# Forty-four in-projections of a hybrid mLSTM, RWKV-7 and S5 step: seventeen beside the RWKV columns, twenty-three behind the last one, four behind the S5 branch's last transposes

## The chip, the cores and the metric

One NeuronCore of one Trainium2 chip runs one launch of the kernel. The metric is the time of the device for that launch in microseconds, the median of three runs: 1379.0 us (1373.04 to 1379.88). Beside the runs there is one execution taken by the hardware profiler. The engines are called PE (TensorE, matrix products), DVE (VectorE), ACT (ScalarE), POOL (GpSimd) and SP (SyncE, whose queue issues all transfers of this kernel). Each engine executes its own instructions in a fixed order.

## The reference, cut to what matters

The layer takes 512 prompt rows and 8 sample rows of width 1024. One combined projection `w_in` gives the columns of three mixers and of three merge gates; each mixer's output is gated, projected, weighted by its merge gate and summed:

```python
z = x @ p['w_in']
xm, ig, fg, og, zm, rcols, zr, u, zs, gm = _split_cols(z)
y_m = (mlstm(xm, ig, fg, og) * silu(zm)) @ p['w_bm']
y_r = (rwkv7(rcols) * silu(zr)) @ p['w_br']
ys  = gelu(s5(u)); ys = ys * sigmoid(ys @ p['s_glu_w'] + p['s_glu_b'])
y_s = (ys * silu(zs)) @ p['w_bs']
g = sigmoid(gm).reshape(b, t, 3, D)
x_new = layer_norm(ALPHA * x + (g[:,:,0]*y_m + g[:,:,1]*y_r + g[:,:,2]*y_s) @ p['w_out'])
```

RWKV-7 updates a matrix state token by token; the kernel computes it in chunks of 64 tokens, with a triangular inverse of each chunk and then eight chunks one behind the other. S5 is a complex diagonal scan in groups of 16 channels. All arrays are float32; outputs are also the new states of each mixer, for prompt and samples.

## The kernel before, in words

The normalised input lies in SBUF as two parts `xh` and `xl` (a rounded part and the rest), 1024 rows deep by 520 columns (512 + 8). One in-projection of 128 columns of `w_in` is `inproj`: it loads a weight tile in two transfers of 256 KB (`wraw`, three buffers), splits it on ACT into `whi` and on DVE into `wlo` (two buffers each), and makes two groups of 24 matmuls into the PSUM tile `g` (three buffers), for 256 and for 264 columns.

The work goes through these stages: entry norm; RWKV; S5 beside the merge of the RWKV branch (`mrg.other(1)`); mLSTM beside the S5 branch's GLU and merge (`mrg.s5()`); the mLSTM branch's merge; the last projection and norm. `interleave` emits two generators in turns.

In-projections whose results are needed only later are called fills. The list `fills` holds them in order, `fill()` takes the first one from it, and each computes a tile in a small pool `fl` (tag `fl`, two buffers) and stores it to DRAM: the S5 input `u` (`fill_u`, to `ud`) or a gate or input column (`fill_z`, tile `zf`, to `zsave`). There are 44: eight of `u`, eight each of `C_OG`, `C_ZS`, `C_ZM` and of the S5 merge gate `C_GM + 2 * D`, two of `C_XM`, two of `C_GM + D`. Later stages look a column up in the dictionary `zsave` and load it, or project it there if it is missing.

RWKV takes 25 columns of its own (`rcol`): one for the low-rank parts, then for each of the eight column tiles a key, a receptance and a value column (8 + ct, ct, 16 + ct). The inner `rcol` calls `e.fill()` ahead of each, so 25 fills are emitted beside these columns. Two column tiles are a pair: `elementwise` for both, then `inverse` (62 DVE operations on the tile `xi`, then small matmuls), then `chain`, eight steps of matmuls (`cr`, `cy`) with DVE and ACT between them, then `headnorm` and the store `ybsave`. Behind the last pair stand the samples' state update and `e.fill(len(e.fills))`, which emits the 19 that remain.

The order of instructions on each engine isn't that of the text alone. A planner with a timeline of its own takes, for each engine, the ready instruction that was emitted first, and waits between engines are added to that order. `tc.issue_after(ins)` adds an edge: what its block emits on the engine of `ins` is queued behind `ins`. Pools of SBUF are stacked from the left, or from the right with `side="right"`; a new pool's tile waits for those tiles that had its place.

S5 works on four parts `pi` of 16 groups; in each, for two halves `j`, two transposes into the PSUM tile `kt` are the last step of making a kernel `ko`, which goes through DMA into `tms`; behind them come `bu`, the scans on DVE, and the `ys` matmuls, whose result is stored to `yssave` and loaded again as `yb` for the GLU (`ysh`, `ysl`).

Of the kernel before, what the change touches and what calls it, by code (L numbers as in the profile page):

```python
# [8 lines left out]
F32 = mybir.dt.float32  # L9
# [6 lines left out]
P = 128  # L16
D = 1024
T = 512
NB = 8
N = T + NB  # L20
KT = D // P
# [11 lines left out]
EH = math.exp(-0.5)  # L33

C_XM, C_IG, C_FG, C_OG, C_ZM = 0, 1024, 1028, 1032, 2056
C_RC, C_ZR, C_U, C_ZS, C_GM = 3080, 6280, 7304, 8328, 9352


@with_exitstack
def hybrid_step(ctx: ExitStack, tc: tile.TileContext, I, O):  # L40
    nc = tc.nc
    V, A, G, TE = nc.vector, nc.scalar, nc.gpsimd, nc.tensor
# [4 lines left out]
    dr = ctx.enter_context(tc.tile_pool(name="dr", bufs=1, space=DRAM))  # L47
# [218 lines left out]
    hmsave = dr.tile([KT, P, N], F32, name="hmsave")  # L266
    ud = dr.tile([KT, P, SL, 80], F32, name="ud")
    flc = ExitStack()
    fl = flc.enter_context(tc.tile_pool(name="fl", bufs=1))
    zsave, fills = {}, []  # L270

    def fill_u(ct):
        us = fl.tile([P, SL, 80], F32, tag="fl", bufs=2, name="us")
# [28 lines left out]

    for ct in range(KT):
        fills.append((fill_u, ct))
    for b, c0 in enumerate((C_OG, C_ZS, C_ZM, C_GM + 2 * D)):
        zd = dr.tile([KT, P, N], F32, name=f"zsave{b}")
        for ct in range(KT):
            fills.append((fill_z, (c0 + ct * P, zd[ct])))

    zx = dr.tile([KT, P, N], F32, name="zsave5")  # L310
    for ct in range(2):
        fills.append((fill_z, (C_XM + ct * P, zx[ct])))

    zd = dr.tile([KT, P, N], F32, name="zsave4")
    for ct in range(2):
        fills.append((fill_z, (C_GM + D + ct * P, zd[ct])))

    def fill(k=1):
        for _ in range(k):
# [39 lines left out]

    env = dict(locals())  # L360
    rwkv(tc, I, O, env)
    flc.close()
    mrg = Merge(tc, I, O, env)
    weng[:] = [V, V]
    mrg.open("mr", 1, 4)
    interleave(s5(tc, I, O, env), mrg.other(1), 1.5)
    mrg.pctx.close()
    weng[:] = [V, V]
    mrg.open("ms", 1, 4)
    interleave(mlstm(tc, I, O, env), mrg.s5(), 0.42)  # L370
    mrg.pctx.close()
    mrg.open("mf", 3, 5)
    for _ in mrg.other(0, ahead=True):
        pass
# [6 lines left out]
def interleave(a, b, n):  # L381

    due = 0.0
    for _ in a:
        due += n
        while due >= 1:
            next(b, None)
            due -= 1
    for _ in b:
        pass  # L390


def rwkv(tc, I, O, env):
    e = type("E", (), env)
    nc = tc.nc
    V, A, G, TE = nc.vector, nc.scalar, nc.gpsimd, nc.tensor
    dma, pa, pc, mm, tr, pcol, inproj, gemm = e.dma, e.pa, e.pc, e.mm, e.tr, e.pcol, e.inproj, e.gemm
    ctx = ExitStack()
    rl = ctx.enter_context(tc.tile_pool(name="rl", bufs=1))
    dr, par, col, epst, shn = e.dr, e.par, e.col, e.epst, e.shn  # L400
# [17 lines left out]
    def rt(name, tag="t", bufs=TB):  # L418
        return rp.tile([P, N], F32, tag=tag, bufs=bufs, name=name)

    def rcol(j):
        rc = rp.tile([P, 1 + N], F32, tag="rc", bufs=1, name="rc")
        e.fill()
        return e.rcol(j, rc, rt("xr"))


# [275 lines left out]
    for s_ in range(4):  # L702
# [11 lines left out]
        for ci in range(2):  # L714
            ct = 2 * s_ + ci
# [6 lines left out]
    for j in range(2):  # L722
        m = 128 if j == 0 else 97
        p = pa("sf")
# [68 lines left out]
    V.tensor_tensor(yst, yst, lng, op=ALU.mult)  # L793
    V.tensor_tensor(bf, bf, yf, op=ALU.add)
    dma(e.ybsave[:, :, T:N].rearrange("c p b -> p c b"), bvs)
    e.fill(len(e.fills))
    ctx2.close()
    ctx.close()
    e.weng[:] = [V, V]
# [145 lines left out]
def s5(tc, I, O, env):  # L945
# [20 lines left out]
    for pi in range(KT // 2):  # L966
# [48 lines left out]
        for j in range(2):  # L1015
            c0 = g0 + 8 * j
            eb = sp.tile([P, 8, SL, SC], F32, tag="eb", bufs=2, name="eb")
            et = sp.tile([P, 8, SL, SC], F32, tag="et", bufs=2, name="et")
            pw = lambda t, q, lo_: t[:, q, lo_:lo_ + SL, c0:c0 + 8].rearrange("p s g -> p g s").unsqueeze(3).to_broadcast(sh)
            bx = lambda q: bb[:, q, 8 * j:8 * j + 8].unsqueeze(2).to_broadcast(sh)  # L1020
            V.tensor_tensor(eb, pw(pf, 0, 0), bx(0), op=ALU.mult)
            V.tensor_tensor(et, pw(pf, 1, 0), bx(1), op=ALU.mult)
            V.tensor_tensor(eb, eb, et, op=ALU.add)
            gm = sp.tile([P, 8, SL, SC], F32, tag="gm", bufs=2, name="gm")
            cx = lambda q: ca[:, j, q].unsqueeze(2).to_broadcast(sh)
            V.tensor_tensor(gm, pw(pf, 0, 1), cx(0), op=ALU.mult)
            gt = sp.tile([P, 8, SL, SC], F32, tag="et", bufs=2, name="gt")
            V.tensor_tensor(gt, pw(pf, 1, 1), cx(1), op=ALU.mult)
            V.tensor_tensor(gm, gm, gt, op=ALU.add)


            p = pa("ko")
            for m in range(4):
                mm(p[32 * m:32 * m + 32, 0:2 * P], ca[:, j, 0, 2 * m:2 * m + 2, :].rearrange("p g c -> p (g c)"),
                   eb[:, 2 * m:2 * m + 2].rearrange("p g s c -> p (g s c)"))
            kt = sp.tile([P, 2, P], F32, tag="w4", bufs=6, name="kt")
            A.activation(kt.rearrange("p h c -> p (h c)"), p[:, 0:2 * P], AF.Copy)
            p = pa("kt")
            for h in range(2):
                tr(p[:, h * P:(h + 1) * P], kt[:, h])  # L1040
            for h in range(2):
                A.activation(ko[:, j].rearrange("p (m h c) -> p m h c", h=2, c=SC)[:, :, h],
                             p[:, h * P:(h + 1) * P].rearrange("p (m h c) -> p m h c", h=2, c=SC)[:, :, h], AF.Copy)
            gms.append(gm)
            ebs.append(eb)
        kf = ko.rearrange("p j c -> p (j c)")
        V.tensor_tensor(kf[0:SC], kf[0:SC], dm.rearrange("p g c -> p (g c)"), op=ALU.add)
        for t in range(SL):
# [695 lines left out]
```

## Time and profile before

| | |
|---|---|
| median of three runs | 1379.0 us |
| the profiled execution | 1378.35 us |
| its span, first to last instruction | 1376.3 us |
| mean granted clock of TensorE | 0.947 of 2.4 GHz |
| PE matmul busy | 1254.4 us, 91% of the span, 10509 instructions |
| PE weight load busy | 1147.4 us, 83% |
| DVE busy | 959.2 us, 70%, 2157 instructions |
| ACT busy | 679.5 us, 49%, 1492 instructions |
| POOL busy | 242.8 us, 18% |
| moved by DMA | 168.49 MB, mean 122 GB/s |

Busy times are unions of the instructions' spans on one engine. Matmuls are pipelined and their ends are modelled, so two that follow each other overlap in the record; how dense they are is read from their starts. The granted clock is 1.0 at 2.4 GHz and 0.5 at 1.2 GHz; a mean between them says for which part of a stretch either held. A wait is put down to the engine and line whose signal came last.

### The profile page before, as it was taken

Reading aid. Unit: us, or ns where it says so; the run is one execution under the profiler, and the core shown is the slowest. Engines: PE = TensorE matmul, PEld = TensorE weight load, DVE = VectorE, ACT = ScalarE, POOL = GpSimd, SP = SyncE. Lnnn points to the kernel's source line nnn. Section 1 sums busy time; section 2 is a strip of 40 time slices with the busy share of each in tenths; the row PEclk is TensorE's granted clock in tenths of the full one; section 3 lists DMA queues with packets and bytes.
Section 4 is the critical chain, followed back from the end, with each engine's and each line's share of the span. In section 5 each row is a group of like instructions: output and inputs, shape, how many; then the busy total and the mean of one; then the engine's idle time right before and its main releaser. Section 6 shows DMA issues by size and latency. Waiting matters only on the chain.

```text
span 1376.3 us, 27658 instructions
## 1 busy us (share of the span) xinstructions
PE 1254.4 (91%) x10509; PEld 1147.4 (83%) x10509; DVE 959.2 (70%) x2157; ACT 679.5 (49%) x1492; POOL 242.8 (18%) x396
## 2 busy tenths in 40 slices
PE   4969999999998999999985988996999999999887
PEld 4969988889897889999865988996989888899855
DVE  6694594569357834768836998995776775555857
ACT  4547657465746674453222332334765774453220
POOL 1402211123122311105200020000000011104600
PEclk8989999999999999999977999997999999999999
DMA  6333332213121312354518444546676866465331
GB/s 185 95 91 109 91 97 64 74 50 87 52 78 46 89 55 85 96 147 141 160 29 149 110 97 104 130 99 179 208 225 207 275 200 203 138 201 189 92 107 62
DMA packets 246707, 168.49 MB, mean 122 GB/s; under 512 B 54808, under 2 KB 222106, under 8 KB 246302
## 3 DMA queue, kind: packets, MB, share of 16 engines
q1 hardware_dynamic: 246574, 166.72, 43.0%
q8 instruction: 83, 1.36, 0.4%
q14 instruction: 50, 0.41, 0.1%
HBM read 125.18 MB, written 39.20 MB: 119 GB/s over the span
## 4 chain that ended last, share of the span: by engine, by line
PE 35%; DVE 7%; DMA 5%; issue 2%; SPq 2%; ACT 1%; POOL 0%; DVEq 0%; ACTq 0%; POOLq 0%
PE g L62 23%; PE qk L62 2%; PE ys L62 2%; DVE wlo L131 2%; SPq L53 2%; PE s L62 1%; DMA wraw<-in_w_bm_dram 1%; PE nd L62 1%; PE pn L62 1%; PE v L62 1%; DMA cn<-in_state_mlstm_c_dram 1%; PE cn L62 1%; DMA wraw<-in_w_out_dram 1%; DMA br<-in_s_b_im_dram 1%; PE cy L62 1%
## 5 line engine op out<-in xcount | busy, mean ns | idle before, releaser
L62 PE MATMUL g<-xh,whi 128*128 128x264 f32 (+1 forms) x1552 | 461.2, 297 | 37.8 <-DVE th L1541 16.0
L62 PE MATMUL g<-xl,whi 128*128 128x264 f32 (+1 forms) x1552 | 457.1, 295 | 2.1 <-DVE xl L217 2.1
L62 PE MATMUL g<-xh,wlo 128*128 128x264 f32 (+1 forms) x1552 | 454.8, 293 | 0.2 <-DVE wlo L131 0.2
L62 PEld LDWEIGHTS g<-xh,whi 128*128 128x128 f32 x1552 | 304.4, 196 | 48.5 <-DVE th L1541 17.0
L62 PEld LDWEIGHTS g<-xl,whi 128*128 128x128 f32 x1552 | 304.2, 196 | 5.3 <-DVE xl L217 2.3
L62 PEld LDWEIGHTS g<-xh,wlo 128*128 128x128 f32 x1552 | 303.6, 196 | 4.4 <-issue 1.1
L130 ACT ACTIVATE whi<-wraw 128x512 fp32r<-128x512 f32 x258 | 151.2, 625 | 201.0 <-PE g L62 154.3
L131 DVE TENSOR_TENSOR wlo<-wraw,whi 128x512 fp32r<-128x512 f32 x258 | 197.5, 788 | 75.4 <-ACT whi L130 72.9
L661 DVE SCALAR_TENSOR_TENSOR xv<-xv,pc,cy 64x64 f32<-64x64 f32 x112 | 31.3, 279 | 28.1 <-PE cy L62 25.3
L62 PE MATMUL g<-ysh,whi 128*128 128x256 f32 (+1 forms) x128 | 39.1, 312 | 11.5 <-ACT ysh L258 9.1
L564 DVE TENSOR_TENSOR lr<-gg,maskg 64x256 f32<-64x256 f32 x32 | 13.5, 422 | 47.4 <-ACT la L563 47.3
L601 DVE TENSOR_TENSOR xi<-xi,itmp 128x31 f32<-128x31 f32 (+15 forms) x124 | 42.7, 344 | 3.0
L62 PE MATMUL g<-w_bmh,wlo 128*128 128x264 f32 (+1 forms) x128 | 37.4, 293 | 7.8 <-DVE wlo L131 7.6
L599 DVE TENSOR_TENSOR itmp<-lu,xi 128x31 f32<-128x31 f32 (+15 forms) x124 | 42.2, 340 | 2.9
L647 POOL COPY xv<-yv 64x128 f32<-64x128 f32 x64 | 24.7, 388 | 109.1 <-PE cr L62 53.8
L62 PE MATMUL g<-w_brh,whi 128*128 128x256 f32 (+1 forms) x128 | 37.4, 295 | 2.8 <-DVE mg L1585 2.6
L62 PE MATMUL g<-ysl,whi 128*128 128x256 f32 (+1 forms) x128 | 39.7, 311 | 0.0
L62 PE MATMUL g<-ysh,wlo 128*128 128x256 f32 (+1 forms) x128 | 39.3, 307 | 0.0
L568 POOL TENSOR_SCALAR_AFFINE_SELECT ar<-ar 64x512 f32<-64x512 f32 x32 | 21.2, 664 | 94.8 <-ACT ar L567 72.8
L62 PE MATMUL g<-bsl,whi 128*128 128x264 f32 (+1 forms) x128 | 37.8, 297 | 0.0
L62 PE MATMUL g<-bsh,wlo 128*128 128x256 f32 (+1 forms) x128 | 37.6, 295 | 0.0
L62 PEld LDWEIGHTS g<-ysh,whi 128*128 128x128 f32 x128 | 26.3, 209 | 13.4 <-ACT ysh L258 9.4
(582 smaller groups left out, 2980.8 us busy)
## 6 DMA issues: line engine op xcount, KB each, us to landing
wraw<-in_w_in_dram SPq DMA_DIRECT2D x194, 256.0 KB
zsave<-zf SPq DMA_DIRECT2D x36, 260.0 KB
cn<-in_state_mlstm_c_dram SPq DMA_DIRECT2D x32, 256.0 KB
out_dram<-cn SPq DMA_DIRECT2D x32, 256.0 KB
yb<-yssave SPq DMA_DIRECT2D x16, 260.0 KB
zz<-zsave SPq DMA_DIRECT2D x16, 260.0 KB
wraw<-in_w_br_dram SPq DMA_DIRECT2D x16, 256.0 KB
wraw<-in_s_glu_w_dram SPq DMA_DIRECT2D x16, 256.0 KB
```

What stands on the lines that cost most here:

```text
L53: nc.sync.dma_start(out, in_)
L62: TE.matmul(out, lhsT, rhs, start=start, stop=stop)
L130: A.activation(hi[:, k, 0:m], raw[:, :, 0:m], AF.Copy)
L131: eng.tensor_tensor(lo[:, k, 0:m], raw[:, :, 0:m], hi[:, k, 0:m].bitcast(F32), op=ALU.subtract)
L564: V.tensor_tensor(lr[hs(pi), pi, u, :], pv[hs(pi), :, 64:128], maskg[hs(pi)].unsqueeze(1).to_broadcast([64, 4, 64]), op=ALU.mult)
L568: G.affine_select(out=z, in_=z, compare_op=ALU.is_ge, fill=0.0, base=-1, pattern=[[0, 4], [1, 2], [1, 64]], channel_multiplier=-1)
L599: V.tensor_tensor(tv, lu[:, s + 1:32, s:s + 1].to_broadcast([P, r, w]), xi[:, s:s + 1, 0:w].to_broadcast([P, r, w]), op=ALU.mult)
L601: V.tensor_tensor(xi[:, s + 1:32, 0:w], xi[:, s + 1:32, 0:w], tv, op=ALU.add)
L647: G.tensor_copy(xv[hs(1 - pi), pi], yv[hs(1 - pi), pi, :, n, :])
L661: V.scalar_tensor_tensor(dst, xv[hs(pi), pi, ci, :], pcs[ci][hs(pi), n:n + 1], psn[hs(pi), ci, :], op0=ALU.mult, op1=ALU.add)
```

## The change

The list of fills gets another order (the two of `C_XM` and the two of `C_GM + D` ahead of the S5 merge gate), and a pattern `PACE` says ahead of which RWKV columns a fill is emitted: ahead of the first, and ahead of two of each tile's three (not of the value column). So 17 are emitted beside the columns, 23 behind the last pair's samples (all but `LATE`), and the last four, which are columns of the S5 merge gate, behind the last step of `mrg.other(1)`, with their PE instructions queued behind the last `kt` transpose of S5. For that the pool `fl` lies on the right side and is closed behind mLSTM rather than behind RWKV.

```diff
+LATE = 4
+PACE = (True,) + 4 * (True, True, False, True, True, False)
...
-    fl = flc.enter_context(tc.tile_pool(name="fl", bufs=1))
-    zsave, fills = {}, []
+    fl = flc.enter_context(tc.tile_pool(name="fl", bufs=1, side="right"))
+    zsave, fills, marks = {}, [], []
...
-    for b, c0 in enumerate((C_OG, C_ZS, C_ZM, C_GM + 2 * D)):
...
+    for c0, k in ((C_OG, KT), (C_ZS, KT), (C_ZM, KT), (C_XM, 2), (C_GM + D, 2), (C_GM + 2 * D, KT)):
+        save(c0, k)
...
     rwkv(tc, I, O, env)
-    flc.close()
     mrg = Merge(tc, I, O, env)
     weng[:] = [V, V]
     mrg.open("mr", 1, 4)
-    interleave(s5(tc, I, O, env), mrg.other(1), 1.5)
+
+    def beside():
+        yield from mrg.other(1)
+        with tc.issue_after(marks[-1]):
+            fill(len(fills))
+        yield
+    interleave(s5(tc, I, O, env), beside(), 1.5)
...
     interleave(mlstm(tc, I, O, env), mrg.s5(), 0.42)
     mrg.pctx.close()
+    flc.close()
...
+    rcols = list(range(24, -1, -1))
+
     def rcol(j):
         rc = rp.tile([P, 1 + N], F32, tag="rc", bufs=1, name="rc")
-        e.fill()
+
+        if PACE[rcols.pop()]:
+            e.fill()
         return e.rcol(j, rc, rt("xr"))
...
-    e.fill(len(e.fills))
+    e.fill(len(e.fills) - LATE)
...
             for h in range(2):
-                tr(p[:, h * P:(h + 1) * P], kt[:, h])
+                last = TE.transpose(p[:, h * P:(h + 1) * P], kt[:, h], e.ident)
...
+            e.marks.append(last.ins)
```

## Rows read from the trace of the kernel before

**Rows 1.** Busy time of each engine, granted clock and DMA by stage.
```profile
core 0: us, PE busy (x) PEld busy (x) DVE busy (x) ACT busy (x) POOL busy (x), PEclk, DMA share, GB/s
80.00:526.00 446.00, 413.44 (x3826) 384.21 (x3824) 287.49 (x682) 285.39 (x661) 97.07 (x206) 0.97 0.26 75
526.00:696.00 170.00, 167.01 (x1606) 155.53 (x1605) 118.81 (x219) 65.36 (x159) 35.49 (x39) 0.99 0.43 126
696.00:725.00 29.00, 19.94 (x159) 13.96 (x157) 8.96 (x27) 9.49 (x26) 3.03 (x6) 0.64 0.10 22
725.00:762.00 37.00, 24.62 (x151) 23.67 (x152) 24.44 (x43) 7.92 (x19) 1.79 (x4) 0.73 0.82 140
762.00:925.00 163.00, 154.56 (x1435) 147.16 (x1436) 155.27 (x302) 56.61 (x120) 15.53 (x22) 0.97 0.50 112
925.00:967.00 42.00, 30.05 (x184) 29.11 (x180) 25.10 (x64) 19.44 (x37) 2.14 (x7) 0.72 0.60 167
```

**Rows 2.** Chain that ended last: start us, us, what; its longest piece.
```profile
1204.46 45.92 PE g L62 x383
```

**Rows 3.** Tiles zf, us, wlo: durations ns min/median/max, first and last start.
```profile
L298 ACT COPY zf<-g x56: 352/372/396, 175.5 to 683.9; 128x256 f32<-128x256 f32 x28, 128x264 f32<-128x264 f32 x28
L53 SPq DMA_DIRECT2D zsave<-zf x36: 338/454/497, 182.0 to 685.6; - x36
...
L53 SPq DMA_DIRECT2D ud<-us x8: 339/410/446, 43.2 to 165.2; - x8
...
L131 DVE TENSOR_TENSOR wlo<-wraw,whi x90: 673/685/716, 93.2 to 525.8; 128x512 fp32r<-128x512 f32 x90
```

**Rows 4.** What PE waited for, 80 to 526: us in total, times, longest.
```profile
PE g L62 <- ACT xr L352: 10.2, 7, 4.2
...
PE iv L62 <- ACT lu L619: 0.3, 1, 0.3
```

**Rows 5.** Stages again: one inverse, and the end of the columns.
```profile
294.00:344.00 50.00, 46.37 (x384) 42.38 (x384) 46.67 (x115) 30.89 (x75) 18.10 (x30) 0.93 0.26 75
...
474.00:526.00 52.00, 49.26 (x515) 45.31 (x513) 27.30 (x56) 36.21 (x82) 8.69 (x18) 0.93 0.22 62
```

**Rows 6.** That inverse, tile xi alone: us, DVE busy, POOL busy, clock, DMA.
```profile
294.00:344.00 50.00, 22.25 (x63) 0.00 (x0) 0.93 0.26 75
```

**Rows 7.** PE in order of time, first matmuls of chain steps: start us, us.
```profile
684.14 0.39 PE L62 MATMUL cr<-xv,ar 128*64 128x64 f32 x5
...
696.46 0.39 PE L62 MATMUL cr<-xv,ar 128*64 128x64 f32 x5
...
700.57 1.01 PE L62 MATMUL cr<-xv,ar 128*64 128x64 f32 x6 [0.52 <-DVE xv L661]
...
706.09 1.01 PE L62 MATMUL cr<-xv,ar 128*64 128x64 f32 x6 [0.51 <-DVE xv L661]
```

**Rows 8.** Tile g alone, the step with fills: PE, PEld, DVE, ACT busy.
```profile
684.00:697.00 13.00, 8.79 (x63) 7.61 (x61) 0.00 (x0) 0.24 (x1) 1.00 0.31 86
```

**Rows 9.** What PE waited for, 696 to 762.
```profile
PE g L62 <- DVE th L1541: 14.9, 3, 6.8
```

**Rows 10.** PE in order of time, end of S5 and start of the GLU.
```profile
913.26 0.38 PE L81 MATMUL kt<-ident,kt 128*128 128x128 f32 x2
...
934.54 0.80 PE L62 MATMUL g<-ysh,whi 128*128 128x256 f32 x2 [3.86 <-ACT ysh L258]
...
954.04 1.01 PE L62 MATMUL g<-ysh,whi 128*128 128x256 f32 x3 [5.21 <-ACT ysh L258]
```

**Rows 11.** SP's queue in order of time, same place.
```profile
941.91 4.30 SPq L53 DMA_DIRECT2D yssave<-yo  x9
...
950.53 0.85 SPq L53 DMA_DIRECT2D yb<-yssave  x2
```

**Rows 12.** SP's queue in order of time, end of RWKV.
```profile
721.50 4.00 SPq L53 DMA_DIRECT2D ybsave<-bv  x2
725.59 0.38 SPq L53 DMA_DIRECT2D pk<-pksave  x1
```

More of the change, by code (lines that the diff above doesn't have):

```diff
@@ L304, in hybrid_step, with save @@
         fills.append((fill_u, ct))
-    for b, c0 in enumerate((C_OG, C_ZS, C_ZM, C_GM + 2 * D)):
-        zd = dr.tile([KT, P, N], F32, name=f"zsave{b}")
-        for ct in range(KT):
+    def save(c0, k):
+        zd = dr.tile([k, P, N], F32, name=f"zsave{c0}")
+        for ct in range(k):
             fills.append((fill_z, (c0 + ct * P, zd[ct])))
[L310 to L316, printed above, removed]
+    for c0, k in ((C_OG, KT), (C_ZS, KT), (C_ZM, KT), (C_XM, 2), (C_GM + D, 2), (C_GM + 2 * D, KT)):
+        save(c0, k)
     def fill(k=1):
```

## The prediction

> **What bounds the kernel now.** I read the stage table first. In it the reader is to see that TensorE (PE) is nearly always busy except at two places: while RWKV column tiles are made (80 to 526 us) PE is busy 413.44 of 446 us, in the stretch behind the last of them (526 to 696 us) 167.01 of 170 us, then 19.94 of 29 us at a granted clock of 0.64 and 24.62 of 37 us at 0.73, and at the end of the S5 branch (925 to 967 us) 30.05 of 42 us at 0.72. In the S5 stage before that, VectorE (DVE) is busy 155.27 of 163 us [rows 1]. So the kernel is bound by PE's queue, with a hole behind RWKV ("hole A", 696 to 762) and one behind S5 ("hole B", 925 to 967).
>
> Second, the price of the thing that is moved. An in-projection is 48 matmuls into tile g. The chain that ended last has 383 of them in one piece of 45.92 us [rows 2], 0.120 us each, so one in-projection is 5.76 us of PE at full clock. Each fill also has two wlo splits of 0.685 us on DVE, two evacuations of 0.37 us on ScalarE, and three transfers on SP's queue; 36 stores of zf and 8 of us make the 44 fills [rows 3].
>
> Third, whether the RWKV stage follows PE. All waits of PE for another engine between 80 and 526 us are 13 rows, of which the largest is 10.2 us in total and the smallest 0.3 us [rows 4]: PE is rarely out of work. But while the 32x32 inverse runs (294 to 344 us is one of the four) DVE is busy 46.67 of 50 us, as long as PE with 46.37 [rows 5], and only 22.25 us of that are the inverse's own operations [rows 6]. There two engines bound at once.
>
> **The change, part by part.** *Fewer fills beside RWKV.* By the code, 25 of the 44 fills are emitted beside the 25 column calls; the new list leaves 17, skipping the one ahead of each value column. Eight fills leave: at PE's price at most 8 x 5.76 = 46.1 us; at least, if DVE set the pace everywhere, 8 x 2 x 0.685 = 11.0 us. The first pair of column tiles has no inverse beside it: two fills in full, 11.5 us. In each of the three later pairs one skipped fill stands in the part that PE bounds (5.76 us) and one beside an inverse, where I take the middle between DVE's price and PE's (1.37 and 5.76), 3.6 us: 3 x 9.36 = 28.1 us. Together 39.6 us, the term I use.
>
> *Four more fills behind the last column tile (23 for 19).* The recurrence then runs its last eight steps, and PE's queue is in order, so a fill between its matmuls delays it. From one step's first matmul to the next is 12.3 us with fills (684.14 to 696.46) and 5.5 us without (700.57 to 706.09) [rows 7]; 63 matmuls of g, 1.31 fills, lie in the former [rows 8]. That is (12.3 - 5.5) / 1.31 = 5.2 us per fill, nearly PE's own price: a fill hides almost nothing there. Three sparse steps are left, which take 3.9 fills at this density, so four fills cost 4 x 5.2 = 20.8 us. Bounds: 23.0 us if nothing is hidden; if all idle time of 696 to 725 us (9.1 us) and all that its clock loses (36% of 19.94, 7.2 us) is used, 23.0 - 16.3 = 6.7 us. I take 20.8, by the steps, the nearest rows. The rest of hole A stays: its largest waits are PE's for th, 14.9 us in three [rows 9], behind RWKV's last store, and no fill is left to run there.
>
> *Four fills tied behind the last transposes of S5.* The tie binds PE alone: these 192 matmuls may not be issued ahead of the last kt transposes, at 913.26 us; behind them in PE's order stand the GLU's matmuls, which now wait at 934.54 (3.86 us) and 954.04 (5.21 us) for ysh [rows 10]. 925 to 967 us has 11.95 us of PE idle, and its clock loses 28% of 30.05, 8.4 us: room for 20.4 of the 23.0 us, so at best the four cost 2.6 us; if none is used, 23.0. Their weights need eight splits (5.5 us) on a DVE that S5 keeps 95% busy, so they will start late in the hole: I let them use two thirds of the room (13.6 us) and take 9.4 us. Within these bounds lies SP: twelve more issues at about 0.4 us, near the 9 stores of yo and the last yb loads, which follow each other from 941.91 to 950.53 us [rows 11]; if they go first, yb is some 5 us later and so is the GLU.
>
> *The fill pool on the other side, closed later.* No instruction is added. S5's first load of pk is issued at 725.59, when SP has finished with the last ybsave store [rows 12], so its memory is not what it waits for; I take nothing. If another neighbour's release came last it could cost one wait such as the 14.9 / 3 = 5 us of [rows 9], or give as much back.
>
> *Which columns go where.* Seven S5-gate fills leave RWKV's stage for the stretch behind it; their evacuation goes to a ScalarE that is busy 65.36 of 170 us there [rows 1] and hides it. Traffic is the same in total; four fills are 3.1 MB (2 x 256 KB and 260 KB each), in a stretch of 42 us whose DMA share is 0.60 at 167 GB/s, 7.0 MB [rows 1]: they would bring it to about 0.86, so they fit.
>
> Sum: 1378.35 - 39.6 + 20.8 + 9.4 = 1368.95 us for the profiled execution (its span of 1376.3 us and 2.05 us around it). The median of the three runs is 0.65 us above that execution, so I forecast 1369.6, rounded to 1369 us.
>
> **The rivals.** *The inverse's DVE sets RWKV's pace, not PE* (slower). DVE runs at 93% in the inverse; if the skipped fill's PE time is only refilled by waiting, each gives back just its splits, 1.37 us: 1378.35 - 11.0 + 20.8 + 9.4 + 0.65 = 1398 us. It decides once a skipped fill gives back under 30.2 / 8 = 3.8 us. For it: [rows 5]; against it: PE's few waits [rows 4], and the first pair, which has no inverse.
>
> *The four late fills miss hole B*, that is, the change doesn't do what it says: the tie is only an earliest place, and their splits may come after S5's last DVE work, beside the GLU, where PE has work anyway. Then they cost 23.0 us: 1378.35 - 39.6 + 20.8 + 23.0 + 0.65 = 1383 us. For it: DVE's 155.27 of 163 us; against it: in the hole itself DVE is busy only 25.10 of 42 us [rows 1].
>
> *Everything fits*: 46.1 us back, 6.7 and 2.6 us paid: 1342 us. Against it: the step rows, where fills hid little.
>
> *The clock.* RWKV's stage runs at a granted clock of 0.97, so PE is at 1.2 GHz for 6% of it, 27 us. The chain steps without fills fell to 0.64 [rows 1]. If thinner filling brought the stage to the 0.93 that 474 to 526 us shows [rows 5], 62 us would be at 1.2 GHz; the 35 more lose half, 17 us: 1387 us. The Trainium skill, page "TensorE: Matmul & The Clock Gate", part 1 ("What's actually happening"), speaks against the change here: the array is throttled by default and activity releases the throttle, so taking matmuls from beside a latency chain can slow those that stay. By that rule the time would be that of this rival; the trace agrees in the uncovered steps (0.64); what fills that are only fewer do, no stretch of it shows.
>
> **How the numbers follow.** Forecast 0.52, with its own range 1357 to 1379 from the three terms' nearer bounds; DVE's pace 0.14; late fills behind the hole 0.14; all fits 0.11; clock 0.09. The range 1345 to 1394 leaves out most of "all fits" and about two thirds of DVE's pace. About 0.5%, 6.9 us, is what can be told from no change: under 1372 lies 0.40 of the forecast, all of "all fits" and 0.02 of others, 0.53; within 0.5% lie 0.12 of the forecast, most of the late-fill case and a third of the clock's, 0.26; slower are DVE's pace and the rest, 0.21.
>
> **What would show it.** Right: the last RWKV column is evacuated some 35 to 45 us before 526; from there to the last ybsave store takes about 20 us longer than the 199 us of now; the wait for ysh in hole B is gone and the clock there near 1.0. Wrong in the first step: column tiles less than 4 us shorter each, with DVE as busy in the inverse as now. Wrong in the second: chain steps of 12 us up to the last but the stretch no longer than before. Wrong in the third: zf evacuations behind glth's first ones. The forecast falls if RWKV's stage gives back under 30 us.

## The result, and the profile after

The changed kernel takes 1396.25 us (median of 4 runs, 1392.24 to 1398.59) against 1378.22 us before (4 runs beside it, 1373.04 to 1379.88): ratio 1.0139, 95% interval 1.012 to 1.0158. It is slower. The forecast of 1369 us was wrong, and the time lies above the range of 1345 to 1394 us.

The stage table of the changed kernel, cut at its own milestones, answers to [rows 1] line by line:

```profile
core 0: us, PE busy (x) PEld busy (x) DVE busy (x) ACT busy (x) POOL busy (x), PEclk, DMA share, GB/s
80.00:518.00 438.00, 385.40 (x3443) 355.47 (x3443) 277.61 (x659) 270.53 (x628) 90.17 (x206) 0.91 0.22 62
518.00:709.00 191.00, 186.01 (x1801) 173.16 (x1800) 126.60 (x237) 75.55 (x177) 35.93 (x43) 1.00 0.42 124
709.00:735.00 26.00, 20.52 (x152) 15.54 (x150) 8.46 (x20) 10.13 (x24) 1.86 (x2) 0.79 0.23 65
735.00:772.00 37.00, 24.68 (x154) 23.72 (x155) 24.81 (x43) 8.49 (x20) 1.77 (x4) 0.73 0.76 140
772.00:930.00 158.00, 154.81 (x1457) 148.33 (x1456) 153.39 (x296) 58.39 (x125) 24.95 (x21) 1.00 0.54 122
930.00:980.00 50.00, 43.05 (x358) 41.52 (x357) 33.70 (x88) 27.40 (x54) 2.80 (x10) 0.90 0.68 197
```

In the RWKV stage 383 matmuls fewer (3826 - 3443, eight fills) made the stage only 8 us shorter. PE is no longer busy nearly all the time there (53 us idle for 33), and its granted clock fell from 0.97 to 0.91. The stretch behind the last column took the four extra fills at full density, and hole A behind it is as it was: PE's three waits for th are 14.6 us (14.9 in [rows 9]).

To add up the difference I follow five events. First in order of time in the kernel before, on ScalarE: the last RWKV column's evacuation, the first of the GLU's glth, the last gate evacuation gt.

```profile
525.66 0.39 ACT L351 ACTIVATE rc<-g 128x264 f32<-128x264 f32 x1
...
960.30 0.45 ACT L1606 ACTIVATE glth<-g,hglub 128x256 f32<-128x256 f32 x1
...
1251.46 0.37 ACT L1559 ACTIVATE gt<-g 128x264 f32<-128x264 f32 x1
```

The same events on ScalarE in the changed kernel:

```profile
517.80 0.37 ACT L348 ACTIVATE rc<-g 128x264 f32<-128x264 f32 x1
...
974.22 0.45 ACT L1614 ACTIVATE glth<-g,hglub 128x256 f32<-128x256 f32 x1
...
1269.57 0.37 ACT L1567 ACTIVATE gt<-g 128x264 f32<-128x264 f32 x1
```

And SP's queue of the changed kernel, S5's first load and the last stores of S5, which answer to [rows 12] and [rows 11]:

```profile
735.87 0.38 SPq L55 DMA_DIRECT2D pk<-pksave  x1
...
951.70 4.32 SPq L55 DMA_DIRECT2D yssave<-yo  x9
```

| stretch | before | after | difference |
|---|---|---|---|
| start to last column's evacuation | 525.66 | 517.80 | -7.9 |
| to pk's load (the stretch behind, and hole A) | 199.93 | 218.07 | +18.1 |
| to the last yssave stores (S5) | 216.32 | 215.83 | -0.5 |
| to the first glth (hole B) | 18.39 | 22.52 | +4.1 |
| to the last gt (GLU, mLSTM) | 291.16 | 295.35 | +4.2 |
| to the end of the span | 124.8 | 123.9 | -0.9 |

The sum is +17.1; the spans differ by 1393.5 - 1376.3 = 17.2 us. So the change paid nearly what was forecast for its costs (18.1 + 4.1 + 4.2 = 26.4 us for 30.2) and got a fifth of what was forecast for its gain (7.9 us for 39.6).

### The profile page after: what moved, and what is told of

It is laid out like the page before. It is cut to its first block, busy times and chain, and to the rows that moved or that the text cites. A ratio compares the mean times of both kernels' runs of the same rounds, so it can differ in the third digit from the quotient of the medians.

```text
span 1393.5 us, 27645 instructions
## 1 busy us (share of the span) xinstructions
PE 1261.2 (91%) x10509; PEld 1151.5 (83%) x10509; DVE 963.9 (69%) x2157; ACT 682.1 (49%) x1492; POOL 245.5 (18%) x396
## 4 chain that ended last, share of the span: by engine, by line
PE 39%; DMA 5%; DVE 5%; ACT 2%; issue 2%; SPq 1%; DVEq 0%; ACTq 0%
PE g L64 27%; PE ys L64 2%; DVE wlo L133 1%; PE pn L64 1%; PE qk L64 1%; PE nd L64 1%; PE s L64 1%; DMA wraw<-in_w_bm_dram 1%; SPq L55 1%; PE cn L64 1%; PE v L64 1%; DMA wraw<-in_w_out_dram 1%; PE bu L64 1%; DMA yb<-bsave 1%; DMA br<-in_s_b_im_dram 1%
## 5 line engine op out<-in xcount | busy, mean ns | idle before, releaser
L64 PE MATMUL g<-xh,whi 128*128 128x264 f32 (+1 forms) x1552 | 465.9, 300 | 41.0 <-ACT xr L349 19.8
L64 PE MATMUL g<-xl,whi 128*128 128x264 f32 (+1 forms) x1552 | 465.2, 300 | 1.9 <-DVE xl L219 1.9
L64 PEld LDWEIGHTS g<-xh,whi 128*128 128x128 f32 x1552 | 309.6, 200 | 50.1 <-ACT xr L349 21.3
L64 PEld LDWEIGHTS g<-xl,whi 128*128 128x128 f32 x1552 | 309.4, 199 | 7.2 <-DVE xl L219 2.2
L64 PEld LDWEIGHTS g<-xh,wlo 128*128 128x128 f32 x1552 | 308.5, 199 | 3.9 <-issue 0.8
L133 DVE TENSOR_TENSOR wlo<-wraw,whi 128x512 fp32r<-128x512 f32 x258 | 205.9, 822 | 70.7 <-ACT whi L132 69.1
L571 DVE TENSOR_TENSOR lr<-gg,maskg 64x256 f32<-64x256 f32 x32 | 13.5, 422 | 39.5 <-ACT la L570 39.4
L64 PE MATMUL g<-w_bmh,whi 128*128 128x264 f32 (+1 forms) x128 | 37.3, 292 | 0.0
L64 PE MATMUL g<-w_bml,whi 128*128 128x264 f32 (+1 forms) x128 | 37.3, 292 | 0.0
L64 PE MATMUL g<-bsh,wlo 128*128 128x264 f32 (+1 forms) x128 | 37.3, 293 | 0.0
L300 ACT COPY zf<-g 128x256 f32<-128x256 f32 (+1 forms) x56 | 20.6, 368 | 33.1 <-issue 18.3
```

The lines of the kernel that those rows point to most:

```text
L64: TE.matmul(out, lhsT, rhs, start=start, stop=stop)
L133: eng.tensor_tensor(lo[:, k, 0:m], raw[:, :, 0:m], hi[:, k, 0:m].bitcast(F32), op=ALU.subtract)
L300: A.copy(z[:, s:s + n], p)
L571: V.tensor_tensor(lr[hs(pi), pi, u, :], pv[hs(pi), :, 64:128], maskg[hs(pi)].unsqueeze(1).to_broadcast([64, 4, 64]), op=ALU.mult)
```

## The experiments

Theory S ("slack theory" in the first expectations, C in the later ones): TensorE is not what the RWKV columns wait for once fills are taken away, because other chains through VectorE and ScalarE are nearly as long. Its rivals: TensorE bounds and its lower clock ate the gain; buffers bound; the new layout or the column order costs something. "Last column" below is always the start of the last rc evacuation of the RWKV columns, and "behind" the time from there to pk's load. Each is read from the one profiled execution of its kernel; the three kernels with 25 fills there and the whole inverse have their last column at 525.7, 526.0 and 526.6 us, the changed kernel and its pacing alone at 517.8 and 518.1 us.

**Each part of the change alone.** All three stand on the changed kernel.

The layout and the column order alone:

```
-LATE = 4
-PACE = (True,) + 4 * (True, True, False, True, True, False)
+LATE = 0
+PACE = 25 * (True,)
...
-        with tc.issue_after(marks[-1]):
-            fill(len(fills))
-        yield
```

> A control: pool on the right side, closed late, and the new order of the fills, but a fill ahead of all 25 columns and none late (25, 19, 0 as before). Every theory that puts the loss on pace and place of the fills expects before's time within 3 us, 1376 to 1382 us. The rival that the pool's new neighbours or the order of the columns cost the time expects 1386 us or more.

Measured: 1377.65 us, ratio 1.0 [0.9985, 1.0015]; last column 526.0, behind 201.2 us. The fill pool's side and the order of the zf columns cost nothing. The pacing alone, with the pattern of the changed kernel:

```
-LATE = 4
+LATE = 0
...
-        with tc.issue_after(marks[-1]):
-            fill(len(fills))
-        yield
```

> The changed kernel with no late fills: 17 beside the columns, 27 behind the last one. If a fill behind the last column costs 4.5 us or more (18.2 us for 4, as the traces say) and the late ones cost about 2 us each, this is some 10 us slower than the changed kernel: about 1406 us. If the holes behind RWKV had room left, it is the same as the changed kernel, 1396 us.

Measured: 1402.76 us, ratio 1.0169 [1.0141, 1.0196]; last column 518.1, behind 230.8 us, from yssave to glth 17.2 us. So pacing alone makes the kernel slower: eight fills give back 526.0 - 518.1 = 7.9 us in front and cost 230.8 - 201.2 = 29.6 us behind. The late fills alone:

```
-PACE = (True,) + 4 * (True, True, False, True, True, False)
+PACE = 25 * (True,)
```

> The changed kernel with a fill ahead of all 25 RWKV columns again, so 25 fills beside the columns, 15 behind them and 4 behind S5's last transposes. After minus before, the traces give RWKV's columns -7.9 us for 8 fills fewer, the stretch from the last column to the first S5 load +18.2 us for 4 fills more, and the S5 end and what follows about +7 us for the 4 late fills. If RWKV's pace is not PE's (slack theory), this version loses nothing in RWKV, wins about 18 us behind it and pays about 7: some 11 us under before, about 1367 us. If PE sets the pace there (the forecast's step), the 25 fills cost their full 46 us against the changed kernel: about 1.0 of it or slower, 1396 us or more. Rival: the tail is not shortened by taking fills from it because its length is set by the samples' DVE work: then 1385 us.

Measured: 1382.05 us, ratio 1.002 [1.0002, 1.0037]. The four fills leave 201.2 - 188.4 = 12.8 us behind the columns and cost 23.1 - 18.3 = 4.8 us up to glth and 297.8 - 293.7 = 4.1 us up to the last gt. By that the profiled execution, the fastest of its ten, is 3.1 us shorter than that of the layout alone (spans 1374.2 and 1377.3 us); by the medians the kernel is 4.4 us longer, in executions that lie between 1376.08 and 1384.55 us. The 1367 us that theory S expected was missed, and so was the 1396 us of TensorE's: the four fills gave 12.8 us for 18 and cost 8.9 us for 7. Moving four fills from one place to the other is close to a wash either way.

**TensorE's part of a fill against the rest of it.** In the first kernel each skipped fill is replaced by its matmuls alone, on data that is already there (and two copies of one column); in the second by its weight loads, splits and evacuations, with two of the 48 matmuls. Neither has the fill's store to DRAM.

```
         if PACE[rcols.pop()]:
             e.fill()
+        else:
+            for s, n in HALVES:
+                ps = e.psg.tile([P, 512], F32, tag="g", name="gd")
+                for q in range(24):
+                    mm(ps[:, 0:n], e.xh[:, q % KT, 0:P], e.xh[:, q % KT, s:s + n], start=(q == 0), stop=(q == 23))
+                sink = rl.tile([P, 1], F32, tag="sink", bufs=1, name="sink")
+                A.copy(sink, ps[:, 0:1])
```

> The changed kernel with 48 matmuls of no use (the normalised input against itself, into the same PSUM tile g, one column of the result copied away by ScalarE) at each of the 8 places where a fill was skipped: PE's share of the fill comes back, its weight load, its splits on DVE and its stores do not. Slack theory: PE was idle there, so the time of the RWKV columns stays at 438 us within 5 and the whole at about 1396 us, with a granted clock back near 0.97. Clock theory (the fall from 0.97 to 0.91 ate the gain of fewer fills): the clock comes back but the matmuls cost what the fills did, 438 to 446 us. PE-throughput (the forecast's step): the columns take up to 46 us more, the whole up to 1440 us. DVE theory: as slack.

Measured: 1398.73 us; the last column is at 517.82 us, as without the dummies. Busy time of the RWKV stage of that kernel (columns as in [rows 1]):

```profile
80.00:518.00 438.00, 414.03 (x3840) 385.36 (x3840) 278.25 (x660) 271.38 (x644) 89.15 (x206) 0.96 0.22 62
```

TensorE carries as many matmuls as before (3840 for 3826), at a clock of 0.96, and the stage has the length of the one with 3443. Matmuls and clock came back together here, so this run alone does not part them. The second kernel:

```
+        else:
+            hi, lo = e.load_w(I["w_in"][0, :, C_ZM:C_ZM + P])
+            sink = rl.tile([P, N], F32, tag="sink", bufs=1, name="sink")
+            for s, n in HALVES:
+                ps = e.psg.tile([P, 512], F32, tag="g", name="gd")
+                mm(ps[:, 0:n], hi[:, KT - 1], e.xh[:, KT - 1, s:s + n], start=True, stop=False)
+                mm(ps[:, 0:n], lo[:, KT - 1], e.xh[:, KT - 1, s:s + n], start=False, stop=True)
+                A.copy(sink[:, s:s + n], ps[:, 0:n])
```

> The changed kernel, with everything of a skipped fill put back except 46 of its 48 matmuls and its store: the two weight loads, the two roundings on ScalarE, the two splits on DVE, two matmuls and two evacuations, all of it useless. It is the counterpart of the run with the dummy matmuls, which gave the last RWKV column at 517.8 us as without them. If ScalarE and DVE with their round trips set the pace of the RWKV columns and PE has slack there (theory S), the last column's evacuation goes back to about 526 us (the 7.9 us that the change gave back were this rest, 1.0 us a fill) and the time is 1396 + 8 = 1404 us. If the rest is free and only a whole fill costs (matmuls and rest together), it stays at about 518 us and the time at 1396 us.

Measured: 1396.98 us, ratio 1.0129 [1.01, 1.0158]; last column 520.18 us. A miss for theory S as I had put it: the rest alone takes back 2.4 of the 7.9 us (while DVE's busy time in the stage rose by 11.2 us, from 277.6 to 288.8), the matmuls alone 0, a whole fill all of it. The prices of the parts do not add up to that of the whole. What in a whole fill makes the difference is not shown: the store was in neither kernel, and 2.4 us is less than the 3.7 us by which the next change, of buffers, moves the last column.

**Buffers and POOL.**

More buffers first:

```
-    TB = 6
+    TB = 7
...
-        rc = rp.tile([P, 1 + N], F32, tag="rc", bufs=1, name="rc")
+        rc = rp.tile([P, 1 + N], F32, tag="rc", bufs=2, name="rc")
```

> The changed kernel with one buffer more for the elementwise tiles t (7 for 6) and two for the column tile rc (1 before). In the changed kernel ScalarE's xr evacuation waits 13.2 us for DVE's ka, 10.9 us for DVE's xr, and PE 19.8 us for the xr evacuation between 80 and 518 us. If these buffers set the pace, most of the last two rows goes and the last column comes 10 to 25 us earlier: 1371 to 1386 us. If the pace is set by the work in front of them (DVE's and ScalarE's serial operations), the waits only move: the last column within 4 us of 518 and 1393 to 1399 us.

Measured: 1398.77 us, last column 521.5 us. The waits moved (PE for the xr evacuation 14.6 us for 19.8), the columns did not come earlier (521.5 us for 517.8). These two kinds of buffers are not the bound; those of the weights (`wraw`, `whi`, `wlo`) and of PSUM were not tried. Then half of the splits on POOL:

```
     gates(tc, I, O, env)
     next(setup, None)
+    e.weng[:] = [V, G]
...
+    e.weng[:] = [V, V]
     e.fill(len(e.fills) - LATE)
```

> The changed kernel with the second of each pair of weight splits on POOL while the RWKV columns run (40 of 80 splits, 0.685 us each, 27 us of DVE's work). If DVE sets the pace of the whole stage, the last column comes some 27 us earlier than 518 us: 1369 us. If DVE does so only beside the inverses (a third of the fills and columns lie there), some 9 us earlier: 1387 us. If the split's way to the first matmul is what counts, POOL's slower split makes the columns later and the time over 1396 us.

Measured: 1402.82 us, the median of three executions, ratio 1.0176 [1.0147, 1.0205]; a fourth took 4562.25 us, for a reason that no trace shows, and is left out. Last column 526.8 us: later by 9 us. The tile wlo on POOL in that kernel between 80 and 527 us, durations in ns min/median/max:

```profile
L133 POOL TENSOR_TENSOR wlo<-wraw,whi x35: 1270/1292/2269, 98.7 to 499.3; 128x512 fp32r<-128x512 f32 x35
```

It takes 1.29 us for DVE's 0.69. The split stands ahead of a column's matmuls, and 7.5 of the 9 us are there already at the end of the first pair, which has no inverse beside it (the transpose of la begins at 170.5 us for 163.0), so I read the loss as the split's own duration. Nor did it free DVE: the inverse's operations became longer beside POOL (last section). So this run takes 34 splits from DVE and yet says little about whether DVE bounds.

**The decisive pair: a shorter inverse, with 17 and with 25 fills.**

Both stand on the kernels of the first block, the paced one (17 fills beside, 27 behind) and the one with the layout alone (25 and 19). The shorter inverse leaves out 20 of the 31 elimination steps, so what it computes is not the inverse; the edit is one line:

```
-        for s in range(31):
+        for s in range(0, 31, 3):
```

> The paced kernel without late fills (17 beside the columns, 27 behind), with 11 of the 31 elimination steps of each 32x32 inverse: 40 of 62 DVE operations of 0.34 us left out, 13.5 us of DVE in each of the three inverses that lie ahead of the last column (40 us), so its output is not the reference's. It stands beside the same paced kernel with the whole inverse: last column at 518.1 us, 1402.8 us. Theory C (several chains of nearly one length: with 17 fills the longest one runs through DVE and ScalarE, PE's own is shorter): the last column comes 20 to 40 us earlier, 480 to 498 us. Theory of a bound by PE still (its lower clock of 0.91 eats what the fills gave back): the last column stays within 6 us of 518 us. The fourth inverse lies behind the last column and can give up to 13 us more there in either.

Measured: 1361.27 us; last column 486.56 us, 31.5 us earlier than the same kernel with the whole inverse (518.1). Busy time of its RWKV stage:

```profile
80.00:487.00 407.00, 377.41 (x3487) 348.01 (x3487) 241.87 (x545) 268.92 (x632) 92.88 (x209) 0.92 0.24 67
```

> The same shortened inverse with all 25 fills beside the columns (19 behind, none late); it stands beside the kernel before and the layout-only one: last column at 526 us, 1378 us. Theory C: with 25 fills PE's chain is the longest by a little, so the same 40 us of DVE give back only part: the last column at 510 to 522 us, less than half of what the kernel with 17 fills gains. If DVE sets the pace by itself in both, the gain is the same in both (20 to 40 us). If PE bounds with 25 fills alone and DVE's work is hidden: under 4 us.

Measured: 1357.38 us; last column 519.22 us, 6.8 us earlier than with the whole inverse (526.0). Busy time of its RWKV stage:

```profile
80.00:519.00 439.00, 416.36 (x3898) 384.94 (x3898) 254.64 (x572) 286.26 (x665) 94.62 (x210) 0.97 0.27 76
```

Tile xi alone, up to the last column, in the changed kernel and in the first of these two:

```profile
80.00:518.00 438.00, 73.31 (x192) 4.43 (x8) 0.91 0.22 62
80.00:487.00 407.00, 31.68 (x72) 4.45 (x8) 0.92 0.24 67
```

The same 41 us of DVE are worth 31.5 us with 17 fills and 6.8 us with 25. And eight fills are worth 519.2 - 486.6 = 32.6 us (4.1 us each) with the short inverse, 7.9 us (1.0 each) with the whole one. Either change alone gives 7 to 8 us, both together 526.0 - 486.6 = 39.4 us. So with 25 fills and the whole inverse two chains of nearly one length hold the columns, one through TensorE's fills and one through DVE's inverse; take away either and the other still stands at 518 to 519 us. (That TensorE's is the longer of the two by a little, as theory C had it, these runs don't show: then the short inverse alone would have given nothing.) Whether the inverse counts by the time in which it keeps DVE from other work, or as a step that later work waits for, they don't part either. The first run also settles the clock: TensorE gets the 17 fills done by 487 us at 0.92, so the 0.91 of the changed kernel is not what held its columns until 518.

**How the price of a fill goes on to both sides.**

One fill beside, without late ones:

```
-PACE = (True,) + 4 * (True, True, False, True, True, False)
+PACE = (True,) + 24 * (False,)
```

> One fill beside the columns and 43 behind the last one, no late ones: how far the RWKV columns come forward when PE has nothing else there. Theory C: what is left is the chain through DVE and ScalarE, which no fill's matmuls lengthen; 16 fills fewer than the changed kernel give back their splits and roundings at most, 16 x 1 us: the last column at 500 to 512 us. If PE's queue still counts, 16 x 5.76 = 92 us: 426 us. The stretch behind grows by 16 x 3.4 to 5.8 us: the whole near 1402 - 16 + 55 to 92 = 1440 to 1480 us.

Measured: 1442.22 us in one execution; last column 486.2 us at a clock of 0.79 in the stage. Both theories miss: 14 us earlier than the near end of C's window, 60 us later than TensorE's. Then 33 beside, without late ones; the list now counts fills:

```
-PACE = (True,) + 4 * (True, True, False, True, True, False)
+PACE = (1,) + 4 * (2, 1, 1, 2, 1, 1)
...
-        if PACE[rcols.pop()]:
-            e.fill()
+        e.fill(PACE[rcols.pop()])
```

> The opposite edit: two fills ahead of each key column, one ahead of every other (33 fills beside the RWKV columns, 11 behind the last one, none late). Theory S, slack not yet used up: eight fills more cost 8 x 1.0 = 8 us beside the columns and take 8 x 3.6 = 29 us from the stretch behind them (3.2 to 4.2 us a fill between the runs with 15, 19, 23 and 27 fills there): 1378 + 8 - 29 = 1357 us, the last column at 534 us. If PE is the bound as soon as anything is added (the slack of 33 us is gone at 25 fills), the eight cost 8 x 5.76 = 46 us less what is idle: the last column at 550 to 572 us and 1375 to 1395 us.

Measured: 1368.21 us, ratio 0.9923 [0.9898, 0.9948]: faster than both kernels, though 11 us over what theory S expected and 7 us under the other case. Last column 541.0 us (8 fills more cost 15 us, 1.9 each), behind 176.9 us (24.3 us less, 3.0 each). And 29:

```
-PACE = (1,) + 4 * (2, 1, 1, 2, 1, 1)
+PACE = (1,) + 4 * (2, 1, 1, 1, 1, 1)
```

> Two fills ahead of every second key column (29 beside, 15 behind, none late), between the 25 fills of before (last column 526 us, 199.9 us from there to pk's load) and the 33 of the run with more (541 us, 176.9 us). The stretch behind should be 188 us as in the run with 15 fills there. Theory C: PE's chain is the longest one from 25 on and each fill costs more as it grows: 526 + 4 x 1.9 = 533.5 us or less, and 1378 + 7.5 - 11.8 = 1374 us; at PE's own price from 25 on (4 x 5.76 = 23 us, less the 33 us idle not used) 1389 us.

Measured: 1374.34 us, ratio 0.9975 [0.9964, 0.9986]; but the last column came at 542.3 us, no earlier than with 33 fills, and behind were 181.1 us for the 188 expected. The time fits the first case; the way there does not. The same with the 48 dummy matmuls of above at the -1:

```
-PACE = (1,) + 4 * (2, 1, 1, 1, 1, 1)
+PACE = (1,) + 4 * (2, 1, 1, -1, 1, 1)
...
-        e.fill(PACE[rcols.pop()])
+        k = PACE[rcols.pop()]
+        e.fill(abs(k))
+        if k < 0:
...
```

> 29 fills beside the columns as in the run before this one, and at the other four key columns 48 useless matmuls each (and two one-column copies) where the run with 33 has its second fill. The run with 29 ended its columns at 542.3 us with a granted clock of 0.965 there, the run with 33 at 541.0 us with 0.996. If the clock pays for the matmuls (PE bounds from 25 fills on, and 4 x 5.76 = 23 us more work of PE are bought with 3% more clock), the clock here is 0.99 or more, the last column lies within 3 us of 541.5 us and the time at 1372 to 1377 us, as with 29 fills. If the clock has no part in it and the places of the doubled fills made 29 slow, four more sets of matmuls cost 10 to 23 us: 552 to 565 us and 1385 to 1398 us.

Busy time of the three RWKV stages (columns as in [rows 1]), one row each: with 29 fills,

```profile
80.00:542.00 462.00, 435.38 (x4011) 406.37 (x4011) 292.84 (x694) 290.76 (x672) 97.06 (x208) 0.96 0.29 79
```

with 29 and the dummies,

```profile
80.00:544.00 464.00, 449.14 (x4186) 418.82 (x4185) 292.33 (x703) 292.35 (x681) 94.57 (x206) 0.99 0.29 79
```

and with 33:

```profile
80.00:541.00 461.00, 446.83 (x4179) 417.28 (x4179) 296.72 (x700) 296.65 (x686) 95.30 (x206) 1.00 0.31 86
```

Last column of the run with dummies 544.3 us, its stage's clock 0.993 (0.965 without them; means of the granted clock over 80 to 541 us): in the stage it came as the clock's theory asked, 192 more matmuls (23 us) cost 2 us. The whole time is 1383.19 us, ratio 1.0046 [1.0029, 1.0063], and not the 1372 to 1377 expected, since behind the columns the profiled execution (the slowest of its ten, 1388.09 us) took 189.5 us, as the run with 15 fills there and none doubled (188.4); why 29 without dummies took only 181.1 stays open. Last, 33 beside, 7 behind and the changed kernel's four late ones:

```
-LATE = 0
+LATE = 4
...
+        with tc.issue_after(marks[-1]):
+            fill(len(fills))
+        yield
```

> 33 fills beside the columns, 7 behind the last one and the changed kernel's four tied to the end of S5. Beside the run with 33, 11 and none late (1368.2 us): four fills fewer behind the columns give 4 x 2.9 = 11.6 us back if the price from 15 to 11 fills there goes on (188.4 to 176.9 us), nothing if the recurrence's own steps are now the bound there; four late ones cost 8 to 11 us as in the two runs that had them. So 1365 to 1368 us, or 1376 to 1379 us.

Measured: 1366.12 us, ratio 0.9922 [0.9903, 0.9941]. Behind 161.0 us (15.9 less); from yssave to glth 23.1 (+3.2), from glth to gt 296.7 (+5.4). It beats both kernels too, but its interval and that of 33 fills without late ones overlap nearly wholly.

| fills beside | inverse | last column, us | clock of the stage | behind: fills | behind: us |
|---|---|---|---|---|---|
| 1 | whole | 486.2 | 0.79 | 43 | 226.7 |
| 17 | whole | 518.1 | 0.91 | 27 | 230.8 |
| 17 (changed kernel) | whole | 517.8 | 0.91 | 23 | 218.1 |
| 25 | whole | 526.0 | 0.97 | 19 | 201.2 |
| 25 (late fills alone) | whole | 526.6 | 0.95 | 15 | 188.4 |
| 29 | whole | 542.3 | 0.96 | 15 | 181.1 |
| 33 | whole | 541.0 | 1.00 | 11 | 176.9 |
| 33 (with late fills) | whole | 541.4 | 0.99 | 7 | 161.0 |
| 17 | short | 486.6 | 0.92 | 27 | 213.0 |
| 25 | short | 519.2 | 0.97 | 19 | 188.1 |

(With one fill, those left over run on into S5, the last of them until 810 us, which is why 43 cost no more than 27 in this column.)

## Why the prediction was wrong

**Step 1 failed: "Eight fills leave" and "Together 39.6 us".** It gave 7.9 us. The prediction took TensorE for the bound in the whole stage, and beside the inverses the middle between DVE's price and TensorE's, because TensorE was busy 413.44 of 446 us and its waits were small. Both rows were right and the conclusion did not follow: they say that TensorE was hardly ever out of work, not how long the next chain is. That one, through DVE's inverse, was of nearly the same length: with eight fills fewer it still ended at 518 us. The prediction's own check ("wrong in the first step: column tiles less than 4 us shorter each, with DVE as busy in the inverse as now") is what came out. One inverse of the changed kernel, busy time of all engines, answers to [rows 5]:

```profile
288.00:338.00 50.00, 42.73 (x332) 37.61 (x332) 45.31 (x116) 26.92 (x65) 14.71 (x30) 0.87 0.22 60
```

and its tile xi alone to [rows 6]:

```profile
288.00:338.00 50.00, 22.46 (x64) 0.00 (x0) 0.87 0.22 60
```

DVE has 45.31 us (46.67 before) in a window of the same length, TensorE 42.73 at a lower clock. The inverse's first and last elimination step begin at 288.8 and 336.4 us here, at 296.5 and 342.6 us in the kernel before: about one fill less (332 matmuls for 384), and the inverse took no less time, 47.6 us for 46.1. By parts: the first pair has no inverse beside it, and there two skipped fills were priced at 11.5 us. The pair's end, the transpose of la with which the inverse begins, lies here in the kernel before,

```profile
169.66 2.07 DVE L589 STREAM_TRANSPOSE lu<-la 128x1024 f32<-128x1024 f32 x1
```

and here in the changed one:

```profile
163.02 2.07 DVE L596 STREAM_TRANSPOSE lu<-la 128x1024 f32<-128x1024 f32 x1
```

6.6 us, 3.3 per fill, so even there other engines follow closely. The six fills of the later pairs were priced at 28.1 us and gave 7.9 - 6.6 = 1.3 us. What TensorE then waits for is spread over the round trips through ScalarE and DVE, the largest of them between 80 and 518 us (us in total, times, longest; [rows 4] before):

```profile
PE g L64 <- ACT xr L349: 19.8, 8, 4.8
PE cr L64 <- DVE rs L659: 5.4, 5, 1.7
PE cy L64 <- DVE yv L662: 5.2, 7, 1.7
```

**The rival that came true** for the changed kernel is "the inverse's DVE sets RWKV's pace, not PE". It was priced at 11.0 us back and 1398 us in all; 7.9 us and 1396.25 us were measured. That the total comes so near is partly luck: it has 3.1 us too much given back and 3.8 us too much paid. It was to decide once a skipped fill gave back under 3.8 us, and a fill gave 1.0. The pair with the shorter inverse shows the mechanism: take DVE's steps away and 8 fills are worth 4.1 us each, near step 1's 39.6 / 8 = 4.95 us. The rival got 0.14 because of the small waits of TensorE and the first pair. One row spoke for it more loudly than I let it: DVE at 93% in the inverse [rows 5], of which there are three ahead of the last column. Its price per fill (two splits) was right in size only: the splits with the rest of a fill brought back 2.4 us in eight, the matmuls alone 0, of the 7.9.

**Step 2 held.** Four fills more behind the last column: forecast +20.8, measured +18.1, 4.5 us a fill for 5.2. The way is the forecast one, too: the last chain steps, 4.1 and 5.5 us apart before, now have fills between them. They begin here:

```profile
689.50 0.39 PE L64 MATMUL cr<-xv,ar 128*64 128x64 f32 x5
...
701.28 0.34 PE L64 MATMUL cr<-xv,ar 128*64 128x64 f32 x4
...
713.90 0.39 PE L64 MATMUL cr<-xv,ar 128*64 128x64 f32 x5
```

They are 11.8 and 12.6 us apart. Over all runs with 7 to 27 fills there the stretch grows from 161.0 to 230.8 us, 3.5 us a fill.

**Step 3 held in size.** Late fills at the end of S5: forecast +9.4, measured 4.1 + 4.2 = 8.3 us; 8.9 us where they were the only change. Half of it came only behind glth's first evacuation, where the working has no term: TensorE is idle 4.8 us between 974 and 1270 us, 1.5 us between 960 and 1252 us before; what holds it there was not followed. Their evacuations on ScalarE lie ahead of glth's first (974.22 us), as the prediction asked:

```profile
941.65 0.36 ACT L300 COPY zf<-g 128x264 f32<-128x264 f32 x1
943.98 0.37 ACT L300 COPY zf<-g 128x256 f32<-128x256 f32 x1 [1.97 <-PE g L64]
...
948.27 0.36 ACT L300 COPY zf<-g 128x264 f32<-128x264 f32 x1
...
953.17 0.37 ACT L300 COPY zf<-g 128x256 f32<-128x256 f32 x1 [1.50 <-PE g L64]
...
957.21 0.36 ACT L300 COPY zf<-g 128x264 f32<-128x264 f32 x1
```

The waits of TensorE for ysh, 3.86 and 5.21 us in [rows 10], shrank to the last two of these rows of PE's waits between 930 and 980 us, and the clock there rose from 0.72 to 0.90:

```profile
PE v L64 <- ACT wvh L260: 4.6, 1, 4.6
PE g L64 <- ACT ysh L260: 1.3, 1, 1.3
PE g L64 <- DVE ysl L262: 0.5, 1, 0.5
```

The first row is new: a wait for a weight of the mLSTM (3.9 to 4.8 us in every run with late fills; without them only the run with one fill beside the columns has it). So the hole was filled but for that wait, and what did not fit in it was paid: the rival "late fills miss hole B" (23.0 us) is out.

**Layout and column order, priced at nothing,** cost nothing: ratio 1.0 [0.9985, 1.0015].

**The clock rival** had the fall right (0.97 to 0.91; it expected 0.93) and its price wrong. The Trainium skill, page "TensorE: Matmul & The Clock Gate", part 1 ("What's actually happening"), says that activity releases a throttle that is there by default; the table agrees (0.79, 0.91, 0.97, 1.00 with 1, 17, 25 and 33 fills; 0.95 in the second kernel with 25 and 0.96 with 29 break the order a little). But with 17 fills TensorE did not set the pace, and the lower clock cost the columns nothing that the runs show: 0.92 was enough to end the columns at 487 us once the inverse was short.

**What stays open.** The price of a fill beside the columns isn't smooth: 2.0 us each from 1 to 17, 1.0 from 17 to 25, 4.1 from 25 to 29, then less than nothing to 33. Part of the last two may be the clock, and part which operations happen to stand behind which in the queues, since the planner may order each of these kernels another way. No run parts these.

## What to carry to other kernels

That an engine is busy and waits little doesn't say how long the next chain is. Before work that is taken off it is priced in full, look for the stretch where a second engine is as busy, and work out the loop that runs through that stretch at the second engine's price as well. The cheap test is to shorten the suspected second chain once with and once without the change: if the change's worth differs (32.6 against 7.9 us here), the second chain was the limit. And where filler work costs less in one stage (1.9 us a fill beside the columns, from 25 to 33) than in the next (3.0 behind), move it into the first one: the opposite of this change gave 1368.21 us, ratio 0.9923 [0.9898, 0.9948].

## What the runs showed of the hardware that was not expected

Useless matmuls were nearly free in a stage in which TensorE is busy 435 of 462 us: with 29 fills the stage ran at a granted clock of 0.965, that is, 7% of it at the lower of the two levels; 192 more matmuls, 23 us at full clock, brought it to 0.993 and the last column from 542.3 to 544.3 us. The gain of clock, 0.028 x 462 = 13 us of full speed, covers a bit over half of those 23 us; most of the rest went into TensorE's idle time, which fell from 26.6 to 14.9 us. Behind the columns the same kernel lost 8 us, so it is no way to save time by itself.

A weight split on POOL takes 1.29 us where DVE needs 0.69, and half of the splits moved there made the columns 9 us later, while DVE's busy time up to the last column stayed as it was (277.6 in 438 us, 276.7 in 447 us) though 34 splits had left it. Its splits went from 48.9 to 29.2 us, but the inverse's operations, the same 186, went from 63.7 to 71.7 us, in the changed kernel

```profile
L608 DVE TENSOR_TENSOR xi<-xi,itmp 128x31 f32<-128x31 f32 (+15 forms) x93 | 32.0, 344 | 2.2
L606 DVE TENSOR_TENSOR itmp<-lu,xi 128x31 f32<-128x31 f32 (+15 forms) x93 | 31.7, 341 | 2.2
```

and with POOL splitting:

```profile
L607 DVE TENSOR_TENSOR itmp<-lu,xi 128x31 f32<-128x31 f32 (+15 forms) x93 | 36.2, 389 | 2.2
L609 DVE TENSOR_TENSOR xi<-xi,itmp 128x31 f32<-128x31 f32 (+15 forms) x93 | 35.5, 381 | 2.3
```

In that run those that overlap an instruction of POOL took 0.49 us on average, those of the same shape that don't 0.35 us (27 shapes). The rest of the 19.7 us went into many smaller groups, part of them operations that now lie ahead of the later last column.
